# Second FFN of a hybrid decoder step: 8 of 22 columns for the prompt beside decode, 14 as block products for all tokens

## The chip, the cores and the metric

The kernel runs on one NeuronCore of one Trainium2 chip, as one program in one launch. The metric is the device time of one execution in microseconds. Five engines work side by side, each through its own queue in order: TensorE (PE, with its weight loads as PEld), VectorE (DVE), ScalarE (ACT), GpSimd (POOL) and SyncE (SP, which here only issues DMAs). PSUM, into which TensorE writes, has banks of 512 fp32 columns for each of 128 partitions.

## The reference, cut to what matters

One layer for 512 prompt tokens and 32 sample tokens (8 sequences of 4) that share all weights. The model width is 1024, the FFN width 2816.

```python
def swiglu(x, wg, wu, wd):
    return (jax.nn.silu(x @ wg) * (x @ wu)) @ wd

def layer(h, ...):
    h = h + 0.5 * rmsnorm(swiglu(rmsnorm(h, norm_g[0]), wg[0], wu[0], wd[0]), norm_g[1])
    m, c_kv, k_r, s_fin = mixer(rmsnorm(h, norm_g[2]), ...)   # HGRN2 heads and latent attention, then @ w_out
    h = h + rmsnorm(m, norm_g[3])
    h = h + 0.5 * rmsnorm(swiglu(rmsnorm(h, norm_g[4]), wg[1], wu[1], wd[1]), norm_g[5])
    return h, c_kv, k_r, s_fin
```

The mixer's attention runs for prompt tokens over the 512 prompt tokens, and for the samples over 4096 cached tokens each, fetched by pages ("decode"). All inputs and outputs are fp32. The change is about the last line but one, the second FFN, and about the product with `w_out` ahead of it.

## The kernel before, in words

Activations stand transposed: 128 features on the partitions, tokens along the free axis, 8 such slabs for 1024 features. A "column" is 128 of the 2816 FFN features, so there are 22. To keep fp32 accuracy with the faster fp32r matmuls every operand is split into a high and a low part, and each product of two 128-row slabs is three matmuls, high by high, high by low and low by high (`mm3`, `gemm`, `gemm_q`). A weight of 128 columns is fetched as `wraw`, split by ScalarE (high, a cast) and VectorE (low, a subtraction) into `wh` and `wl` (`weight`, L250 and L251), and used by 24 matmuls for each group of tokens.

The stages in order:

- First FFN (to about 385 us). The tokens are two halves of 272 (`even`). Columns 0 to 3 are made plainly (`classic`). From then on two columns at a time are made by `seven`: gate (or up) of two columns for two token halves, with the 1024 features in two parts, is a 2 by 2 by 2 block product that takes seven block products in place of eight, 84 matmuls in place of 96, at the price of sums of weight blocks (L609 to L615), sums of token blocks (`T1` to `T4`, made once, L685) and sums of results (`plus`, L627). Finished columns are multiplied with `w_down` in steps of `down`, which `fill` puts between the block products.
- Mixer projections and the HGRN heads, then attention of the prompt in two halves of 256 queries. The prompt's first half is projected with `w_out` (`project(0)`) between the attention heads. The tokens are here two parts of 256 and 288 (`halves`): the second has 256 prompt tokens and the 32 samples.
- Decode. `decode()` walks through 16 half sequences; for each it gathers pages by indirect DMA on POOL's queue into seven slots, transposes them on VectorE (L1381), makes scores on TensorE in 64x32 tiles (L1393), takes the softmax, and multiplies with the values in column groups of 32 (L1426). Between two of its steps the generator `gb` is advanced: it is `ffn(1, 5, (0,), ...)`, the second FFN of the first 256 tokens, all 22 columns in four groups, gate, up and then down.
- After decode, `decode_end` merges the parts of the softmax and finishes the samples' attention (L1494 to L1515). Then `project(1)` projects the other 288 tokens with `w_out`, with the rest of `gb` between its columns, and `gB`, a second `ffn(1, 5, (1,), ...)`, makes the 22 columns for these 288 tokens, fetching and splitting all its weights a second time. `Finish` turns the prompt part back to rows and stores it.

The order of each engine's instructions is made when the program is built. A planner takes the instructions in the order in which they are traced as their priority, models when each is ready, and puts on every engine the first one that is; `tc.issue_after` holds an instruction behind a named one on the same engine. So a generator that is advanced later has a lower priority, and fills gaps that the planner sees.

The lines that the change touches:

## Time and profile before

| what | value |
|---|---|
| time, median of 3 runs | 1250.78 us (1250.63 to 1252.65) |
| span of the profiled execution | 1241.4 us; the trace gives no other time of its own |
| TensorE busy | 1215.0 us, 98% |
| VectorE busy | 982.7 us, 79% |
| ScalarE busy | 738.8 us, 60% |
| mean granted TensorE clock | 0.999 |
| DMA traffic | 195.59 MB, mean 158 GB/s |

The span goes from the first to the last instruction of one profiled execution; the device time is some 9 us longer. "Busy" is time in which at least one instruction of the engine is under way, so pipelined matmuls count once. In lists of groups the columns are: line, engine, operation, output tile `<-` input tiles, shapes, count, busy time in us, mean length in ns, idle time ahead of them and what ended it. Tiles of the `act` pool are named by their slot (`ha`, `mb`, `uha`), whatever stands in them.

### The profile page before, as it was taken

Reading aid. Unit: us, or ns where it says so; the run is one execution under the profiler, and the core shown is the slowest. Engines: PE = TensorE matmul, PEld = TensorE weight load, DVE = VectorE, ACT = ScalarE, POOL = GpSimd, SP = SyncE. Lnnn points to the kernel's source line nnn. Section 1 sums busy time; section 2 is a strip of 40 time slices with the busy share of each in tenths; the row PEclk is TensorE's granted clock in tenths of the full one; section 3 lists DMA queues with packets and bytes.
Section 4 is the critical chain, followed back from the end, with each engine's and each line's share of the span. In section 5 each row is a group of like instructions: output and inputs, shape, how many; then the busy total and the mean of one; then the engine's idle time right before and its main releaser. Section 6 shows DMA issues by size and latency. Waiting matters only on the chain.

```text
span 1241.4 us, 29997 instructions
## 1 busy us (share of the span) xinstructions
PE 1215.0 (98%) x12366; PEld 1151.3 (93%) x12366; DVE 982.7 (79%) x1976; ACT 738.8 (60%) x1559; POOL 76.5 (6%) x80
## 2 busy tenths in 40 slices
PE   8999999999999999999999999999999999999997
PEld 6999999999999989988898888888888999999997
DVE  7897788878678888786877899999998778566665
ACT  7675545455366744545758766666656776554455
POOL 0000000000000000000001312322310000000000
PEclk9999999999999999999999999999999999999999
DMA  6232333232264213333233868878776635545451
GB/s 238 86 115 90 103 103 102 86 99 91 62 221 147 82 54 105 88 94 130 85 105 117 339 214 303 310 282 323 258 275 232 198 106 188 184 137 188 150 151 60
DMA packets 73113, 195.59 MB, mean 158 GB/s; under 512 B 12336, under 2 KB 27728, under 8 KB 68240
## 3 DMA queue, kind: packets, MB, share of 16 engines
q1 hardware_dynamic: 64512, 150.47, 37.3%
q0 software_dynamic: 7168, 41.95, 9.2%
q8 instruction: 97, 1.59, 0.5%
q10 hardware_dynamic: 1296, 1.26, 0.3%
q14 instruction: 40, 0.33, 0.1%
HBM read 183.97 MB, written 9.67 MB: 156 GB/s over the span
## 4 chain that ended last, share of the span: by engine, by line
PE 79%; DVE 11%; ACT 7%; issue 2%; DMA 2%; SPq 0%; DVEq 0%; ACTq 0%
PE acc L259 29%; PE acc L277 13%; PE dn L259 8%; PE Y L575 7%; PE X L575 4%; PE Z L575 4%; DVE kh L1381 3%; PE acc L731 3%; DVE wl L251 2%; ACT wh L250 1%; PE s L1393 1%; ACT pbuf L1417 1%; DMA wraw<-w_g 1%; PE pa L952 1%; PE o L1426 1%
## 5 line engine op out<-in xcount | busy, mean ns | idle before, releaser
L250 ACT CAST wh<-wraw 128x1024 fp32r<-128x1024 f32 (+2 forms) x194 | 185.0, 957 | 164.3 <-PE acc L259 103.7
L251 DVE TENSOR_TENSOR wl<-wraw,wh 128x1024 fp32r<-128x1024 f32 (+2 forms) x194 | 214.6, 1108 | 72.2 <-ACT wh L250 71.6
L277 PE MATMUL acc<-uha,wh 128*128 128x256 f32 (+1 forms) x528 | 155.5, 295 | 0.1
L277 PE MATMUL acc<-uha,wl 128*128 128x256 f32 (+1 forms) x528 | 150.0, 285 | 0.8 <-DVE wl L251 0.7
L277 PE MATMUL acc<-ula,wh 128*128 128x256 f32 (+1 forms) x528 | 150.5, 286 | 0.0
L259 PE MATMUL acc<-uhb,wh 128*128 128x288 f32 (+1 forms) x432 | 128.0, 296 | 0.0
L259 PE MATMUL acc<-uhb,wl 128*128 128x288 f32 (+1 forms) x432 | 127.0, 295 | 1.0 <-DVE wl L251 0.8
L259 PE MATMUL acc<-ulb,wh 128*128 128x288 f32 (+1 forms) x432 | 127.5, 295 | 0.0
L277 PEld LDWEIGHTS acc<-uha,wh 128*128 128x128 f32 x528 | 99.2, 188 | 8.8 <-issue 7.9
L277 PEld LDWEIGHTS acc<-uha,wl 128*128 128x128 f32 x528 | 99.2, 188 | 2.3 <-DVE wl L251 1.6
L277 PEld LDWEIGHTS acc<-ula,wh 128*128 128x128 f32 x528 | 99.4, 188 | 1.6 <-issue 1.2
L259 PEld LDWEIGHTS acc<-uhb,wl 128*128 128x128 f32 x432 | 81.2, 188 | 1.6 <-DVE wl L251 1.6
L259 PEld LDWEIGHTS acc<-uhb,wh 128*128 128x128 f32 x432 | 81.0, 187 | 0.2 <-ACT uhb L170 0.2
L259 PEld LDWEIGHTS acc<-ulb,wh 128*128 128x128 f32 x432 | 81.1, 188 | 0.1
L259 PE MATMUL dn<-hh,dh 128*128 128x272 f32 x256 | 74.3, 290 | 0.0
L259 PE MATMUL dn<-hh,dl 128*128 128x272 f32 x256 | 73.7, 288 | 0.0
L259 PE MATMUL dn<-hl,dh 128*128 128x272 f32 x256 | 73.6, 288 | 0.0
L277 PE MATMUL acc<-uhb,wh 128*128 128x272 f32 x176 | 52.8, 300 | 0.0
L1417 ACT COPY pbuf<-pt 32x64 f32<-32x64 f32 x192 | 46.5, 242 | 10.1 <-DVE pt L1413 7.3
L259 PE MATMUL acc<-hlb,wh 128*128 128x288 f32 x176 | 52.1, 298 | 0.0
L259 PE MATMUL acc<-hhb,wh 128*128 128x288 f32 x176 | 51.8, 298 | 0.0
L1393 PE MATMUL s<-kh,q 64*32 64x128 f32 x2560 | 48.0, 273 | 3.5 <-DVE kh L1381 3.5
(632 smaller groups left out, 3881.3 us busy)
## 6 DMA issues: line engine op xcount, KB each, us to landing
wraw<-w_u SPq DMA_DIRECT2D x66, 512.0 KB, 4.3
wraw<-w_g SPq DMA_DIRECT2D x65, 512.0 KB, 3.9
wraw<-w_d SPq DMA_DIRECT2D x40, 384.0 KB, 3.5
wraw<-w_in SPq DMA_DIRECT2D x24, 512.0 KB, 3.5
wraw<-w_d SPq DMA_DIRECT2D x32, 320.0 KB, 3.1
wraw<-w_d SPq DMA_DIRECT2D x16, 512.0 KB, 3.8
wraw<-w_o SPq DMA_DIRECT2D x16, 512.0 KB, 3.7
g_S<-state SPq DMA_DIRECT2D x4, 512.0 KB, 4.4
```

What stands on the lines that cost most here:

```text
L250: nc.scalar.copy(wh[:, :kt], w[:, :kt])
L251: nc.vector.tensor_tensor(wl[:, :kt], w[:, :kt], f32(wh[:, :kt]), op=ALU.subtract)
L259: nc.tensor.matmul(out, a, b, start=n == 0, stop=n == last)
L277: nc.tensor.matmul(acc[:, :n], a[:, k], b[:, k], start=k + i == 0, stop=k == kt - 1 and i == 2)
L575: nc.tensor.matmul(bank, a[p][:, k], b[q][:, k], start=first and k + n == 0, stop=k == 3 and n == 2, skip_group_check=True)
L731: nc.tensor.matmul(accs[x, d], wts[d][p][:, k], hs[k // 2][q][:, k % 2, x], start=k + n == 0, stop=k == nf - 1 and n == 2)
L952: nc.tensor.matmul(po[es, c].rearrange("p (n m) -> p n m", m=m), kx[:, cs], up(qx[:, cs], m), start=True, stop=True, skip_group_check=True)
L1381: nc.vector.transpose(kh[:, g].rearrange("p a j k -> p a (j k)"), src)
L1393: nc.tensor.matmul(self.s[r][c * 32 : c * 32 + 32, :P], q[rs, j], kh, start=st + jj == 0, stop=st == len(JS) - 1 and jj == 1, skip_group_c ...
L1417: (nc.scalar.copy if g else nc.vector.tensor_copy)(self.p[g * 32 : g * 32 + 32, c // 2, c % 2 * 4 : c % 2 * 4 + 4, self.i * 16 : self.i * ...
L1426: nc.tensor.matmul(o[g : g + 32, :R], self.p[:, c, a], self.craw[c][:, a], start=i + c == 0 and a < 4, stop=i + c == 2 and a >= 4, skip_gr ...
```

## The change

The second FFN is cut by columns, not by token halves.

- Columns 0 to 7 are made for the 512 prompt tokens beside decode, by the new generator `phase_a`. It starts with `project(1)` for the prompt's second half of 256, makes column 0 for each half by itself, and the others with 512 tokens in one matmul. After four columns their share of down is made, copied from PSUM by ScalarE and stored to DRAM (`mA[0]`, `mA[1]`). The pace is given by `PRE` (two or three steps for each of the first ten decode steps) and then one step for each; it was 100 steps spread evenly.
- The samples' `w_out` and columns 0 to 7 are made apart, in plain fp32, by `rowprod`: the 32 samples are the stationary operand, four weights go through four column groups at once. Their weights come by `rows4` on POOL's DMA queue, unsplit, 2 MB at a time into two slots. `w_out` is done in `decode_end`, the columns in `sample_cols`, which is advanced after each piece of the later columns.
- Columns 8 to 21 are made for all 544 tokens, after decode, in halves of 272 with the block products of the first FFN, which are now a function `block_ffn` for both: columns 8 and 9 plainly, 10 to 21 by `seven`. The token sums T1 to T3 are made from the split u. The gate's result is multiplied with the norm's factor in `gated`.
- The sums of down are put together by DMA: `mA[0]` is loaded into `mT`, `mA[1]` and the parked sums of columns 8 to 11 (`mA[2]`) are added to it by accumulating DMAs on POOL's queue.
- `Finish` works on the second half of 272 (240 prompt tokens as two overlapping blocks of 128, and the samples); the first 272 tokens are stored transposed.
- Outputs of the prompt's attention are split into high and low as they are made (`oo`) instead of ahead of `project`; the four-buffer rotation of `wh` and `wl` becomes two buffers.

```diff
-FCH = (((0, 6), (6, 6), (12, 6), (18, 4)), ((0, 6), (6, 6), (12, 5), (17, 5)))
+FA, CA = 8, 4
...
-NW, WX = 2, 2
-NDEC = 100
+NW = 2
+PRE = (2, 2, 2, 2, 2, 2, 2, 2, 3, 3)
...
+    def block_ffn(i, B, r=None):
+        b11, b21, b22, t1, t2, t3, t4 = B
...
         def gated(H, G, V, i):
             z = G[:, 2 * i : 2 * i + 2]
             t = mk([P, 2, W2], F32, "sit", 2)
+            if r is not None:
+                nc.vector.tensor_tensor(z, z, r, op=ALU.mult)
             sigmoid(t, z)
...
+    def phase_a():
...
+        def gate(f):
+            s = mk([P, TP], F32, "sil", 2, pool=ffa)
+            z = yield from col(wt(w_g, f), f)
+            yield
+            swish(s, z, full)
+            return s
+
+        def up(f, s):
+            z = yield from col(wt(w_u, f), f)
+            yield
+            nc.vector.tensor_tensor(s, s, z, op=ALU.mult)
+            split(hh[:, f % CA], hl[:, f % CA], s)
+
+        def downs(c):
+            for d in range(KD):
+                acc = yield from gemm_q(weight([wcols(w_d[1], c * CA, CA, d * P)], CA), (hh, hl), 2)
+                t = mk([P, TP], F32, "sit", 2, pool=ffa)
+                nc.scalar.copy(t, acc)
+                nc.scalar.dma_start(mA[c][:, d], t)
+                yield
+
+        acc = squares(0)
+        pj = project(1, oo[1], to_ffn, ffa)
+        next(pj)
...
-                nc.scalar.copy(oT[x][:, NH + hd, : 2 * P], o[:, : 2 * P])
+                split(*[t[:, NH + hd] for t in oo[x]], o[:, : 2 * P])
...
-        slots = ("ulb", "uhb", "ha", "hb", "mb", "q0", "dx")
+        slots = ("ma", "dx0", "dx1", "mb", "ha", "hb", "q0")
...
+        def rows4(w, d0, n, slot):
+            out = []
+            for i, sl in enumerate(slot):
+                t = qt[:, : 2 * KD * P] if sl == "q0" else mk([P, 2 * KD * P], F32, sl, pool=act)
+                t = t.rearrange("p (i k c) -> p i k c", i=2, k=KD)
+                nc.gpsimd.dma_start(t, w[d0 + 2 * i : d0 + 2 * i + 2, :, :n].rearrange("i p k c -> p i k c"))
+                out += [t[:, 0], t[:, 1]]
+            return out
+
+        def rowprod(a, raws):
+            o = ps("sr")[:, :P]
+            for k in range(KD):
+                for g in range(4):
+                    nc.tensor.matmul(o[g * TS : (g + 1) * TS], a[:, k], raws[g][:, k], start=k == 0, stop=k == KD - 1, skip_group_check=True)
+            return o
...
+            wo = [rows4(w_o, 0, KD, ("ha", "hb")), rows4(w_o, 4, KD, ("q0", "ma"))]
...
+            tok = tmp("rs_t", 2 * P)
+            for r in range(2):
+                nc.scalar.copy(tok[:, r * P : (r + 1) * P], rowprod(oTs, wo[r]))
+                yield
...
+            split(u4[0][:, :, TP:], u4[1][:, :, TP:], uS)
...
+        def sample_cols():
+            uS, uR = smp
+            z = tmp("rs_t", 2 * P)
+            for r in range(2):
+                nc.scalar.copy(z[:, r * P : (r + 1) * P], rowprod(uR, rows4(w_g[1], 4 * r, KD, ("ma", "mb"))))
+                yield
...
         ga, gn = decode(), decode_new()
-        na, ib = len(JS) * (NH2 + 2) + 4, 0
-        for ia in range(na):
+        for ia in range(len(JS) * (NH2 + 2) + 4):
             next(ga)
             if ia % 2:
                 next(gn, None)
-            while ib * na < (ia + 1) * NDEC:
+            for _ in range(PRE[ia] if ia < len(PRE) else 1):
                 next(gb)
-                ib += 1
         for _ in ga:
             pass
-        decode_end()
+        for _ in decode_end():
+            for _ in range(2):
+                next(gb, None)
...
+        def tile_pair(j, src, C, mid=None):
+            if j == J0:
+                ws = [wsplit(w) for w in raw_pair(src, 2 * j)]
+                for x in BOTH:
+                    classic(ws, C, x, ucol)
+                    next(sc, None)
+                if mid:
+                    mid()
+            else:
+                seven(raw_pair(src, 2 * j), C, mid)
+                next(sc, None)
...
+            if j == 7:
+                mT = [actslot("m", x, n=W2) for x in BOTH]
+                for i in range(2):
+                    for x in BOTH:
+                        n = min(even[x].stop, TP) - even[x].start
+                        (nc.gpsimd.dma_start if i else nc.sync.dma_start)(mT[x][:, :, :n], mA[i][:, :, even[x].start : even[x].start + n], **({"accum_op": ALU.add} if i else {}))
+            if j == 8:
+                fill(99)
+                owed[0] = 0
+                for x in BOTH:
+                    nc.gpsimd.dma_start(mT[x], mA[2][:, :, even[x]], accum_op=ALU.add)
+            tile_pair(j, w_g[1], G)
+            if j == J0:
+                X, Y, Z = (mk([P, 4, W2], F32, n, 3) for n in ("hh", "hl", "hh"))
+                for o, b in ((X, B12), (Y, B11)):
+                    nc.vector.tensor_tensor(o, f32(b[0]), f32(b[1]), op=ALU.add)
+                nc.vector.tensor_tensor(Y, X, Y, op=ALU.subtract)
...
+            def rest():
+                if j > J0:
+                    gated(H, *late, 1)
+                if j in (6, 8):
+                    fill(99)
+                    owed[0] = 0
+                    downs.append(down(j - 2, hs, park if j == 6 else add_m))
+
+            tile_pair(j, w_u[1], V, rest)
```

More of the change, by code (lines that the diff above doesn't have):

```diff
@@ L586, in fill, with down @@
                     downs.pop(0)
[L588 removed]
+        def down(q0, hs, sink):
             nf = 2 * len(hs)
@@ L784, in project @@
             nc.scalar.copy(mT[:, d], acc)
             scale_sq(sacc, mT, d, gv, 3)
+        d0 = 0
+        if pool:
+            for d, acc in enumerate((yield from gemm_2([wo(d) for d in range(2)], o))):
+                column(d, acc)
+            d0 = 2
+            yield
+        for d in range(d0, KD):
+            column(d, (yield from gemm_q(wo(d), o, 4)) if pool else gemm(wo(d), o))
             yield
         yield from post(x, mT, sacc, None, nxt)
+    u4 = []
+    hs2 = dr.tile([P, KD, T], F32, name="hs2", tag="hs2")
```

595 lines of the change are left out of this document (329 added, 266 removed).

## The prediction, made before the changed kernel was run

> **What bounds the kernel now.** I read the page's busy times and chain first, then one row for each stage, then the spacing of TensorE's instructions by width.
>
> ```profile
> span 1241.4 us, 29997 instructions
> PE 1215.0 (98%) x12366; PEld 1151.3 (93%) x12366; DVE 982.7 (79%) x1976; ACT 738.8 (60%) x1559; POOL 76.5 (6%) x80
> PE 79%; DVE 11%; ACT 7%; issue 2%; DMA 2%; SPq 0%; DVEq 0%; ACTq 0%
> ```
>
> The stages (columns: time, busy time and count of PE, PEld, DVE, ACT, POOL, granted clock, DMA share, GB/s) are the first FFN, mixer and HGRN, attention, decode, and the tail after decode.
>
> ```profile
> 5.00:385.00 380.00, 379.37 (x2990) 374.22 (x2991) 303.63 (x557) 216.16 (x407) 0.56 (x1) 1.00 0.35 115
> 385.00:573.00 188.00, 187.65 (x1932) 171.29 (x1931) 151.51 (x354) 100.14 (x222) 1.88 (x8) 1.00 0.30 91
> 573.00:698.00 125.00, 118.70 (x867) 109.72 (x866) 94.84 (x229) 89.50 (x208) 8.47 (x8) 1.00 0.43 144
> 698.00:951.00 253.00, 248.28 (x4463) 218.39 (x4465) 237.73 (x522) 159.37 (x419) 64.06 (x58) 1.00 0.78 276
> 951.00:1241.40 290.40, 281.04 (x2124) 277.70 (x2124) 194.23 (x315) 171.42 (x304) 1.35 (x1) 0.99 0.51 158
> ```
>
> TensorE sets the end in every stage: it is idle 4.7 us of the decode stage and 9.4 us of the tail. The change touches these last two, 543 us of the span. VectorE is second: 94% in decode, 67% in the tail.
>
> A busy matmul overlaps the next, so its mean length isn't its price. The price is the spacing: the time of a stretch of one kind over its count (windows, then steps of the chain of waits).
>
> ```profile
> 609.00:614.30 5.30, 5.30 (x25) 4.33 (x24) 4.54 (x8) 5.11 (x9) 0.00 (x0) 1.00 0.38 129
> 100.00:300.00 200.00, 200.00 (x1591) 199.32 (x1590) 158.24 (x291) 101.93 (x192) 0.00 (x0) 1.00 0.31 96
> 1040.00:1220.00 180.00, 180.00 (x1347) 179.45 (x1347) 111.38 (x163) 94.90 (x153) 0.00 (x0) 1.00 0.52 160
> ...
> 954.33 8.75 PE acc L277 x73
> ...
> 753.97 1.86 PE o L1426 x32
> 763.09 1.52 PE s L1393 x96
> ```
>
> 288 wide (second half of the tokens): 180/1347 = 0.1336 us. 272 wide (first FFN): 200/1591 = 0.1257. 256 wide: 8.75/73 = 0.1199. 512 wide: two of the 25 were under way when the window opened, so 5.30/23 = 0.2304; its bounds are 5.30/25 = 0.212 and twice the 256 wide, 0.240. Column groups in fp32 (four at a time, 32 columns each) with 256 moving columns: 32 in 1.86 us. The sample products move 128: between half of that, 0.93, and the whole. The 64x32 products of L1393 do move 128, eight at a time, 96 in 1.52; four at a time that is 1.01 for 32. I take 1.0.
>
> **What the change removes and adds on TensorE.** Removed: the first half's 22 columns, 22 x 8 x 3 = 528 matmuls each for gate, up and down, 1584 x 0.1199 = 189.9 us; the second half's 1584 and the 192 of its output projection, 1776 x 0.1336 = 237.3. Together 427.2.
>
> Added beside decode: output projection of the second prompt half 192 x 0.1199 = 23.0; first column by halves 96 x 0.1199 = 11.5; the other seven columns 7 x 2 x 24 = 336 and eight columns of down, 2 x 8 x 4 x 3 = 192, 528 x 0.2304 = 121.7. Added after decode: columns 8 and 9 plainly, 192; twelve block products of 84 in place of 96, 1008; down of 14 columns, 14 x 8 x 2 x 3 = 672; 1872 x 0.1257 = 235.3. Samples: eight products of 32 matmuls, two each for w_out, gate, up and down, 8.1, and about 2 for sums and turns. Together 401.6. **Net -25.6 us.** Twelve saved matmuls in each of twelve pairs x 0.1257 are 18.1 of it; wide matmuls, even halves and samples left out of eight columns are the rest.
>
> **The decode stage.** The groups by line over 700 to 955 us, and a window:
>
> ```profile
> L251 DVE TENSOR_TENSOR wl<-wraw,wh 128x1024 fp32r<-128x1024 f32 (+2 forms) x64 | 70.0, 1096 | 10.7 <-ACT wh L250 10.4
> L336 DVE TENSOR_TENSOR sil<-sil,sit 128x256 f32<-128x256 f32 x19 | 7.9, 421 | 2.5 <-ACT sit L322 2.1
> L392 DVE TENSOR_TENSOR ma<-ma,acc 128x256 f32<-128x256 f32 x16 | 6.4, 402 | 0.0
> ...
> 712.00:951.00 239.00, 234.40 (x4350) 205.10 (x4346) 223.89 (x493) 149.97 (x398) 56.15 (x53) 1.00 0.77 273
> ```
>
> VectorE loses 64 weight splits (70.0), four operations of each of 19 columns (4 x 7.9 = 31.6) and 6.4 of sums; it gains 24 splits of 1024 at 1.22 and 16 of 512 at 0.69 (rows below) = 40, four 512-wide operations in each of eight columns, 22, and about 17 of the projection. That is 29 less, so up to 4.7 us of TensorE's idle time could go; I take 2 (0 to 4.7). Fetched bytes fall as well. Against it: 22 steps now run before the first scores, and the second prompt half waits for the projection's norm, about 11 us of VectorE and ScalarE in series behind 48 matmuls (5.8) of the other half. I take +2 (0 to 6). The extra split of each attention output moves from the tail into the attention stage; its eight pieces of some 0.4 us hide beside TensorE there, or add at most 3.
>
> **The samples' chain.** Decode ends now with a chain that other matmuls cover (timeline, then chain):
>
> ```profile
> 951.51 0.70 PE L1494 MATMUL pb<-q,ones 128*128 128x256 f32 x2
> 953.70 0.63 PE L1434 MATMUL o<-q,q 128*128 128x32 f32 x4 [0.91 <-ACT q L1429]
> 954.59 0.22 DVE L1435 COPY q<-o 128x64 f32<-128x64 f32 x1
> ...
> 963.08 1.82 PE o L1514 x16
> ```
>
> L1494 stands later in the program than L1434 and runs before it: the planner orders each engine by readiness, so independent matmuls can be put into gaps. The chain takes 964.9 - 951.5 = 13.4 us. Behind it now come two w_out products, a turn, two norms and the split of u: 2.0 plus some 16 dependent steps of about 0.5, estimated from the 0.22 to 0.70 above, 10 us. Cover: the last five steps of down, 30 x 0.2304 = 6.9; columns 8 and 9 of the first 272 tokens, which hold no sample, 96 x 0.1257 = 12.1; the chain's own matmuls 4. So 23.4 against 23.0. I take 2; without the 12.1, because the planner leaves them behind, 12.
>
> **The block stage's first pairs.** By form, from 40 to 380 us, where the first FFN does the same:
>
> ```profile
> L171 DVE TENSOR_TENSOR sl<-wraw,sh 128x512 fp32r<-128x512 f32 x36 | 23.6, 686 | 0.7
> L609 DVE TENSOR_TENSOR S<-wraw 128x512 f32<-128x512 f32 x18 | 12.3, 685 | 0.0
> L627 DVE TENSOR_TENSOR ha<-Y,tq 128x272 f32<-128x272 f32 x27 | 11.7, 434 | 0.8 <-PE Y L575 0.8
> L657 DVE TENSOR_TENSOR ha<-ha,sit 128x544 f32<-128x544 f32 x22 | 15.9, 722 | 4.9 <-ACT sit L322 4.9
> L685 DVE TENSOR_TENSOR ma<-ma,mb 128x1088 f32<-128x1088 f32 x1 | 1.3, 1280 | 0.0
> L251 DVE TENSOR_TENSOR wlx<-wraw,whx 128x1024 fp32r<-128x1024 f32 x2 | 2.4, 1218 | 0.0
> ...
> 60.70:71.50 10.80, 10.80 (x86) 10.63 (x85) 9.27 (x16) 10.24 (x20) 0.00 (x0) 1.00 0.27 100
> 71.50:83.00 11.50, 11.50 (x94) 11.50 (x93) 11.27 (x22) 7.88 (x16) 0.00 (x0) 1.00 0.29 93
> ```
>
> A block product costs TensorE 84 x 0.1257 = 10.6 us and VectorE 11 x 0.685 + 5 x 0.434 = 9.7, and the gate now has a fourth operation, for the norm: 4 x 0.72 = 2.9. That is 12.6 against 10.6 wherever no down runs beside it. The two windows show such a pair in the first FFN: VectorE 20.5 of 22.3 us, TensorE without a gap. In the new stage three and a half products in a row have no down. Before them the token combinations (12 operations x 1.28 = 15.4) can start only when the samples are in. From that point VectorE has 15.4 + 3.5 x 9.7 + 4 x 2.9 = 61; TensorE 12.1 + 3.5 x 10.6 + 6.1 of sample products = 55. I take 6 us; 0 if work prepared ahead covers it, 14 if the combinations, 12.8 to the one that the second block wants, aren't covered. After that down (1.5 us a step against 0.8 of VectorE) restores TensorE's lead.
>
> **The sample weights and the parked sums.** POOL's queue now carries the 4 MB of w_out and six loads of 2 MB into the same two slots, each issued only after the product before it has read them; the accumulating loads of the parked sums stand behind these. From the DMA view:
>
> ```profile
> hb<-hsp SPq DMA_DIRECT2D x1, 1152.0 KB, 9.0
> ...
> ha<-hs SPq DMA_DIRECT2D x1, 1024.0 KB, 5.7
> ...
> hb<-pool_c,idx POOLq DMA_INDIRECT x4, 9.4
> ```
>
> 1 MB lands in 5.7 to 9.4 us beside other traffic; two at once I put at 9. The program leaves 48 matmuls, 6.0 us, between the first four sample products, so three of them can be 3 us late; TensorE runs in order, and the block products behind a late one wait. I take 3 (0 to 15). The Trainium skill's "DMA: Bandwidth & Descriptors" (Anatomy of one DMA) fits one such transfer at 2.0 us plus its bytes over 436 GB/s; 2 MB would be an estimated 6.8 us by it, and the three waits 2 us together, not 9. The rows above are slower than the page. The accumulating loads have a whole block product ahead of their first reader: 1 (0 to 6). The last columns and the finish keep their form: no change.
>
> **Sum.** 1241.4 - 25.6 + 2 - 2 + 2 + 6 + 3 + 1 = 1227.8 of span. The trace shows no own time beside the span; the median of the runs, 1250.78, is 9.4 above it, which I add: **1237 us**.
>
> **Rivals.** *All of it arrives.* The planner hides every new wait, as it did in the first FFN (379.37 of 380.00 busy): 1250.8 - 25.6 - 2 = 1223. Against it: combinations that can't start before the samples. *Decode keeps its own pace.* If VectorE and the gathers, not TensorE, pace the scores (94% busy speaks for it), the 33 us of projection and first column, 15 us of them more than ran there before, come ahead of a decode that isn't shorter: 1237 + 15 = 1252, no change. Against it: 29 us less on VectorE. *The sample columns pace the tail* (slower). Sixteen MB come through two slots in series; if the planner believes them earlier than they land and sets them ahead of the block products, w_out's second half and the first four products wait about 6 us each (9 + 3 of turnaround - 6.0), 30, and the uncovered chain costs 10 more. Less the 5 that my sum has for both: 1237 - 5 + 40 = 1272; it decides from 16 us of such waits over my sum on. For it: the order is fixed at build time. Against it: four slots of w_out come free before decode ends.
>
> By "TensorE: Matmul & The Clock Gate" (What's actually happening) of the Trainium skill, an idle window of some 3.4 us halves the clock until a busy one follows. The trace grants 1.00 in all but the tail's last microseconds, so it doesn't show this; after each long wait of the slower rival it would add an estimated 1.7 us.
>
> **How the numbers follow.** A measurement of this kernel tells 0.2%, 2.5 us, from no change. My forecast, 1227 to 1247: 0.56. All of it arrives: 0.15. Decode keeps its pace: 0.09. The sample columns pace the tail: 0.20. Faster 0.71, same 0.09, slower 0.20. The range goes from 1221, all saved with decode's idle time gone, to 1257, where half of the slower rival's waits occur.
>
> **What would show it.** Right: the decode stage ends 3 to 10 us earlier; a spacing near 0.126 in the block stage; TensorE idle 8 to 15 us between the last attention value and the second block pair, with VectorE as releaser; a tail of 265 to 280 us in place of 290. Wrong: waits of TensorE on the sample weights over 10 us together, a decode stage over 253 us, or 512-wide matmuls spaced above 0.24.

## The result, and the profile after

The changed kernel is slower: 1267.99 us (1267.38 to 1269.21) against 1251.72 us for the kernel before on the same chip, a ratio of 1.0125 (95% interval 1.0108 to 1.0142). The forecast was 1237, a ratio of 0.989.

From the page of the profiled execution (span, engines, chain):

```profile
span 1265.6 us, 29473 instructions
PE 1223.2 (97%) x12244; PEld 1122.7 (89%) x12244; DVE 981.6 (78%) x1992; ACT 703.3 (56%) x1524; POOL 91.2 (7%) x102
PE 79%; DVE 10%; ACT 5%; DMA 4%; issue 2%; SPq 0%; DVEq 0%; ACTq 0%
```

That execution took 1267.38 us, 1.8 above its span. So the 9.4 us that the prediction laid around the span was no cost of the program. On four other chips, which ran all the experiments, the kernel before takes 1243.5 to 1244.6 us, some 2 to 3 above the 1241.4 of its profile: so that profile was very likely taken on a chip of their speed, and the first chip is 0.6% slower. The changed kernel was therefore profiled again on one of the four (span 1256.5, time 1258.28; the run e5 below). This second profile stands beside the one of before from here on, and the forecast for such a chip reads 1227.8 + 1.8 = 1229.6 us against a measured 1258.4. Some 29 us are missing. One run of e4 (1476.46 us at a mean granted clock of 0.75) and one of the kernel before (1303.85 us at 0.849) stand apart from all others and are left out of the comparisons.

The stages of the second profile (columns as in the prediction: time, PE, PEld, VectorE, ScalarE, POOL, granted clock, DMA share, GB/s), then the stretches in which time is lost:

```profile
5.00:385.00 380.00, 379.66 (x2984) 374.73 (x2985) 302.43 (x554) 215.35 (x406) 0.92 (x3) 1.00 0.35 115
385.00:573.00 188.00, 187.66 (x1934) 171.45 (x1932) 151.67 (x354) 100.81 (x223) 1.53 (x6) 1.00 0.30 90
573.00:701.00 128.00, 124.32 (x917) 116.17 (x913) 99.86 (x238) 89.93 (x205) 4.92 (x5) 1.00 0.37 114
701.00:955.50 254.50, 241.85 (x3893) 183.45 (x3893) 209.72 (x467) 146.53 (x403) 69.42 (x67) 0.99 0.75 262
955.50:1256.50 301.00, 282.17 (x2524) 273.99 (x2523) 214.94 (x378) 148.55 (x287) 15.70 (x17) 0.97 0.52 159
...
701.00:748.20 47.20, 40.15 (x276) 36.56 (x275) 37.32 (x72) 31.87 (x69) 10.18 (x8) 0.93 0.83 293
748.20:955.50 207.30, 201.70 (x3618) 146.89 (x3618) 172.40 (x395) 114.67 (x334) 59.24 (x59) 1.00 0.73 255
955.50:1000.00 44.50, 42.23 (x461) 38.51 (x461) 34.42 (x49) 17.12 (x33) 3.46 (x5) 0.88 0.55 193
1000.00:1151.00 151.00, 144.04 (x1309) 141.03 (x1308) 109.25 (x194) 80.75 (x157) 10.85 (x12) 0.99 0.68 197
...
703.90:710.70 6.80, 5.04 (x22) 4.78 (x23) 6.16 (x15) 4.25 (x11) 5.11 (x4) 0.50 1.00 344
973.50:983.70 10.20, 9.87 (x43) 9.73 (x44) 7.86 (x11) 2.46 (x6) 0.00 (x0) 0.50 0.26 84
```

The same places before: attention to the first score, the first score to the last value, the chain after decode.

```profile
698.00:711.50 13.50, 13.37 (x109) 12.93 (x107) 13.33 (x30) 8.90 (x21) 7.91 (x5) 1.00 0.83 310
711.50:951.50 240.00, 235.40 (x4360) 205.56 (x4359) 224.39 (x493) 150.97 (x400) 56.15 (x53) 1.00 0.77 273
951.50:1000.00 48.50, 47.53 (x373) 46.78 (x370) 35.16 (x62) 34.70 (x67) 0.00 (x0) 1.00 0.68 223
```

Decode itself is shorter, 207.3 us in place of 240.0. But it starts 36.7 us later, and the tail is 301.0 in place of 290; the forecast's tail was 265 to 280. TensorE's idle time and its clock name three places. What a stretch at half clock costs is read from the spacing of the matmuls in it: 256-wide ones start 0.213 us apart there and 0.120 elsewhere, 272-wide ones 0.227 and 0.126. From 701 to 748 TensorE is idle 7.05 us and runs 6.8 us at half clock; the 20 matmuls of `project(1)` in that stretch lose some 1.9 us. After decode it is idle 2.3 and has 10.2 us at half clock, in which 28 wide and 16 narrow matmuls lose some 4.4. In the block stage (1000 to 1151) it is idle 7.0, and a stretch of 3.4 us from 1130.6 on, right behind a wait, costs some 1.5. Before, the first of these places cost 0.1 us and the second 1.0, and the clock was full until the last microseconds.

### The profile page after: what moved, and what is told of

It is laid out like the page before. It is cut to its first block, busy times and chain, and to the rows that moved or that the text cites. A ratio compares the mean times of both kernels' runs of the same rounds, so it can differ in the third digit from the quotient of the medians.

```text
span 1265.6 us, 29473 instructions
## 1 busy us (share of the span) xinstructions
PE 1223.2 (97%) x12244; PEld 1122.7 (89%) x12244; DVE 981.6 (78%) x1992; ACT 703.3 (56%) x1524; POOL 91.2 (7%) x102
## 4 chain that ended last, share of the span: by engine, by line
PE 79%; DVE 10%; ACT 5%; DMA 4%; issue 2%; SPq 0%; DVEq 0%; ACTq 0%
PE acc L246 19%; PE acc L228 11%; PE dn L228 10%; PE Y L447 8%; PE Z L447 6%; PE X L447 5%; PE s L1391 3%; PE acc L627 3%; PE acc L1800 2%; PE o L1424 2%; DVE kh L1379 1%; DMA wraw<-w_u 1%; PE pa L957 1%; DMA wraw<-w_g 1%; ACT pbuf L1415 1%
## 5 line engine op out<-in xcount | busy, mean ns | idle before, releaser
L246 PE MATMUL acc<-uh,wh 128*128 128x272 f32 (+2 forms) x496 | 161.1, 325 | 0.7 <-ACT uh L195 0.7
L246 PE MATMUL acc<-ul,wh 128*128 128x272 f32 (+2 forms) x496 | 155.7, 315 | 0.7 <-DVE ul L196 0.7
L246 PE MATMUL acc<-uh,wl 128*128 128x272 f32 (+2 forms) x496 | 155.3, 314 | 0.5 <-DVE wl L220 0.5
L220 DVE TENSOR_TENSOR wl<-wraw,wh 128x1024 fp32r<-128x1024 f32 (+2 forms) x80 | 86.2, 1078 | 35.8 <-ACT wh L219 33.4
L219 ACT CAST wh<-wraw 128x1024 fp32r<-128x1024 f32 (+2 forms) x80 | 74.8, 935 | 67.1 <-PE acc L246 49.3
L228 PE MATMUL dn<-hh,dh 128*128 128x272 f32 x384 | 111.4, 290 | 0.0
L228 PE MATMUL dn<-hh,dl 128*128 128x272 f32 x384 | 110.5, 288 | 0.0
L228 PE MATMUL dn<-hl,dh 128*128 128x272 f32 x384 | 110.5, 288 | 0.0
L246 PEld LDWEIGHTS acc<-uh,wh 128*128 128x128 f32 x496 | 93.2, 188 | 14.1 <-issue 9.1
L246 PEld LDWEIGHTS acc<-uh,wl 128*128 128x128 f32 x496 | 93.1, 188 | 7.0 <-issue 1.3
L246 PEld LDWEIGHTS acc<-ul,wh 128*128 128x128 f32 x496 | 93.3, 188 | 6.2 <-issue 1.2
L228 PEld LDWEIGHTS dn<-hh,dh 128*128 128x128 f32 x384 | 72.3, 188 | 1.0 <-issue 0.2
L228 PEld LDWEIGHTS dn<-hl,dh 128*128 128x128 f32 x384 | 72.5, 189 | 0.0
L228 PEld LDWEIGHTS dn<-hh,dl 128*128 128x128 f32 x384 | 72.1, 188 | 0.0
```

Source lines behind the costliest of these rows:

```text
L219: nc.scalar.copy(wh[:, :kt], w[:, :kt])
L220: nc.vector.tensor_tensor(wl[:, :kt], w[:, :kt], f32(wh[:, :kt]), op=ALU.subtract)
L228: nc.tensor.matmul(out, a, b, start=n == 0, stop=n == last)
L246: nc.tensor.matmul(acc[:, :n], a[:, k], b[:, k], start=k + i == 0, stop=k == kt - 1 and i == 2)
```

## The experiments

All runs are compared with the kernel before on the same chip. Times of different chips stand side by side below, because the kernel before agrees on these chips within 1.2 us. The expectations of e1 to e4 count from the first chip's 1267.99, so their differences are what is compared. The 95% intervals reach 1.4 to 3.8 us to either side, and by the ratios the gains come out up to 3.5 us smaller than by the medians; a gain below some 4 us is therefore not told from none. Executions of one kernel differ in part by their clock: e1's four take 1249.94 us at a mean granted clock of 0.995, 1252.58 and 1254.57 at 0.992, and 1257.66 at 0.990.

### A control, and cover for the samples' chain

e5 is the changed kernel as it is.

> The changed kernel itself, beside the runs of the kernel before on the chip that ran the first four experiments' fellow kernels, because the two profiles come from chips that differ (the kernel before took 1251.7 us on the one and 1243.5 on the other). Theory (the change's own losses, independent of the chip): 1.0125 times the kernel before, between 1.010 and 1.015. Rival (a good part of the loss belongs to the first chip, whose decode bursts show gaps of 0.59 us): 1.006 or less.

1258.44 us, ratio 1.0107 (1.0089 to 1.0125). The loss belongs to the kernel and not to the first chip.

e1 keeps some ten steps of `gb` back for the time of the samples' chain:

```diff
-            for _ in range(PRE[ia] if ia < len(PRE) else 1):
+            for _ in range(PRE[ia] if ia < len(PRE) else int(ia % 8 < 7)):
```

> Edit: after the first ten decode steps one step in eight is skipped, so about ten more steps of the first eight columns (14 us of TensorE) are left for the samples' chain after decode. Theory A (TensorE runs dry in the samples' chain, and its clock is halved there for 10 us): decode ends about 14 us earlier, the chain gets no longer, the half clock after decode goes; 8 to 14 us less than the changed kernel, 1254 to 1260. Rival B (the chain's length isn't what costs; the sample products and their loads are): the same work only moves, 1266 to 1269.

1253.57 us, ratio 1.009 (1.0068 to 1.0111), 4.9 below the changed kernel by the medians and 2.1 by the ratios, whose intervals overlap. The mechanism of theory A is seen below, its 8 to 14 us are not. The chain of the second profile (start, duration, what) shows what was missing there:

```profile
956.87 6.82 PE acc L246 x29
963.69 1.71 PE o L1553 x16
965.40 3.63 PE sr L1492 x128
969.03 0.27 PE tp L1498
```

The 30 wide matmuls of down that were left, 6.8 us, ran before the chain's first long step. None was left beside the norms, and the first product of columns 8 and 9 (`acc`, L228), on which the prediction had counted for cover, started only after it, at 973.8 us, ended by the split of its own weight:

```profile
968.96 0.33 PE L1498 MATMUL tp<-ident,rs_t 128*128 128x128 f32 x1
969.44 0.33 PE L1498 MATMUL tp<-ident,rs_t 128*128 128x128 f32 x1 [0.15 <-ACT rs_t L1558]
970.25 1.97 PE L1507 MATMUL pr<-s_post,ones 128*128 128x32 f32 x16 [0.47 <-ACT s_post L1563]
973.83 0.60 PE L228 MATMUL acc<-uh,sh 128*128 128x272 f32 x1 [1.62 <-ACT sh L158]
```

With e1's extra steps in the chain the clock stays whole, in the profiled execution, which is the fastest of the four:

```profile
943.00:990.00 47.00, 45.47 (x434) 38.93 (x426) 27.46 (x40) 20.48 (x39) 2.81 (x4) 1.00 0.72 250
```

### The clock by itself

e8 puts eight matmuls that nobody reads into each of six steps of the chain:

```diff
-        for _ in decode_end():
+        for n, _ in enumerate(decode_end()):
...
+            if n > 1:
+                dm = ps("dm", "pm")
+                for i in range(8):
+                    nc.tensor.matmul(dm[:, :256], u4[0][:, i, :P], u4[1][:, i, :256], start=i == 0, stop=i == 7)
```

> Adds eight matmuls of 256 columns, whose result nobody reads, to each step of the samples' chain at decode's end, so that TensorE is not quiet for long; 64 or so in all, 0.12 us each, some 8 us if none of them fell into idle time. Theory 1 (after decode TensorE runs at half the granted clock for 10.2 us, and it is the quiet chain that halves it): the granted clock stays at 1.00 through the chain, and the time is 0 to 5 us below the changed kernel although work was added. Theory 2 (the chain's dependencies set the time, the clock doesn't matter): 0 to 8 us above the changed kernel with the clock at 1.00.

```profile
963.00:1000.00 37.00, 36.41 (x474) 33.89 (x474) 27.59 (x35) 13.68 (x29) 3.51 (x5) 1.00 0.48 156
```

The clock is 1.00 through the chain, so it is the quiet chain that halves it. The time is 1261.60 us, 3.2 more, which is in the range of the second theory. Up to the first block product the 48 dummies (about 48 x 0.12 = 5.8 us) cost about as much as the clock gave back: it starts 57.1 us after the last value against 56.8 (both read from the trace). The rest is lost behind it:

```profile
1000.00:1155.00 155.00, 145.34 (x1298) 142.41 (x1297) 108.85 (x193) 79.51 (x154) 10.06 (x10) 0.97 0.66 192
```

In the block stage TensorE is now idle 9.7 us in place of 7.0, and three stretches of 3.4 us run at half clock in place of one. Why the waits there grew is open. Dummy work didn't pay here; cover should be work that must be done anyway, as in e1, though e1's gain isn't clear of the intervals.

### The start of decode

Two edits of the scores' order and of weight buffers came first. e2 spreads the score groups over the steps:

```diff
-RUNS = {2: (0, 1, 2), 4: (3, 4)}
+RUNS = {1: (0,), 2: (1,), 3: (2,), 4: (3, 4)}
```

> Edit: the five score groups of a half sequence stand behind four decode steps (1, 1, 1 and 2) in place of two (3 and 2). Theory D (with 512-wide matmuls, six instructions a step, a burst of 64 score records outruns what TensorE's sequencer has queued, and it waits about 0.3 us three times a half): the scores' slots fall from 59.6 to about 50 us, 6 to 10 us less than the changed kernel, 1258 to 1262. Rival (the pauses are waits for transposes on VectorE): they stay, 1266 to 1269.

1259.93 us, 1.0136 (1.0118 to 1.0154): no time is won. The gaps of 0.59 us inside the score bursts, at which the edit aimed, stand in the first chip's profile (16 of them); in the second profile of the same kernel the bursts wait in six places, 3.9 us in all, and with e2 nowhere. Losing these waits didn't shorten the program.

e3 gives every third `w_out` weight of `project(1)` a buffer of its own, in the slot of `hl`, which is idle then:

```diff
+            home = None
+            if pool and d % 3 == 2:
+                t = mk([P, 2, 8, P], F32R, "hl", pool=pool)
+                home = t[:, 0], t[:, 1]
-            return weight([wcols(w_o, 0, KD, d * P)], KD)
+            return weight([wcols(w_o, 0, KD, d * P)], KD, home=home)
```

> Edit: every third weight of the second half's output projection gets a buffer of its own (the slot of hl, idle then), three in place of two. Theory A1 (the start of decode loses about 16 us because two weights are held until the last attention output is in, and the next can't be split): TensorE's idle time from 701 to 750 us falls from 7 to 3 or 4 us, the half clock there goes as well, 4 to 8 us less than the changed kernel, 1260 to 1264. Rival (the wait is for the attention output, the norm of the second half, or the 2 MB through the one q0 slot): no more than 1 us, 1267.

1255.37 us, 1.011 (1.0079 to 1.014). The interval covers the changed kernel's ratio. TensorE is idle 4.9 us from 701 to 749 in place of 7.05; of the waits below the one of 1.73 us goes, the others stay, and so does the half clock. In the second profile these gaps, and the waits of the gathers from 701 to 748 us (engine, line, what it waited for, total, times, longest), are:

```profile
704.70 0.77 PE L1331 MATMUL b<-ident,q 128*128 128x128 f32 x2 [1.95 <-DVE mxs L1322]
706.85 0.58 PE L246 MATMUL acc<-ha,wl 128*128 128x256 f32 x1 [0.96 <-DVE wl L220]
719.91 0.39 PE L246 MATMUL acc<-ha,wl 128*128 128x256 f32 x1 [1.73 <-DVE wl L220]
...
POOL ma L1364 <- ACT uh L195: 23.5, 1, 23.5
POOL hb L1364 <- PE acc L246: 18.7, 1, 18.7
```

The gathers find no room: `ma` holds the projection of the first half until its norm (`uh`, L195) is through, `ha` and `hb` hold the second half's attention output until `project(1)` has read it, and `q0` holds its residual. This is why the 22 steps of `PRE` stand beside the first ten decode steps, ahead of the first scores. TensorE has little besides them to do: from 701 to 748 it waits 3.2 us for their weights, 1.4 for the second half's norm and 2.0 for a maximum of the samples' own scores (L1322).

e9 leaves `PRE` empty, one step for each decode step:

```diff
-PRE = (2, 2, 2, 2, 2, 2, 2, 2, 3, 3)
+PRE = ()
```

> One step of the projection and first columns per decode step from the start on, in place of the 22 steps ahead of the first scores; 12 steps are then left beside the samples' chain. Theory 1 (these 22 steps, run without anything beside them, are what empties TensorE at the start of decode): first score 15 to 25 us earlier than at 748 us, less than 4 us of idle TensorE between attention and first score, no half clock after decode; 8 to 12 us less than the changed kernel. Theory 2 (the start waits for what stands before it, the norm of the first half and the slots of the gathers, whatever the order): the idle time at the start stays near 10 us and only the cover of the chain is won, 4 to 5 us less.

1248.68 us, 1.0037 (1.0024 to 1.0049), 9.8 below the changed kernel. In this order the gathers put their rows over the second half's residual and attention output before these are read, so the second prompt half comes out as something else; its time is that of an order for which buffers are lacking. e13 is the nearest one that has room: `ha` and `hb` are gathered into at the same decode step as before, when the 15 steps have run that read them, and `q0` five decode steps later.

```diff
-PRE = (2, 2, 2, 2, 2, 2, 2, 2, 3, 3)
+PRE = (1, 1, 1, 1, 1, 2, 2, 2, 2, 2)
...
-                    if n < 3 and st == 0:
+                    if n < 4 and st == 0:
...
-                        gather(2 + n // 2)
+                        gather(2 - n // 3)
```

> One projection or column step per decode step for the first five, two for the next five, then one; the seventh block's gather moves five decode steps back, behind the last reader of its buffer. Seven steps are left for the samples' chain. Theory 1 (the 22 steps ahead are the cause): first score 15 us or more before 748, 6 to 9 us less than the changed kernel, no half clock after decode. Theory 2 (only the cover counts): 3 to 5 us less.

1251.69 us, 1.0067 (1.0051 to 1.0084), 6.8 less than the changed kernel. From the last attention product to the first score, decode, and after it:

```profile
701.00:731.00 30.00, 26.20 (x182) 24.88 (x183) 22.73 (x44) 21.61 (x46) 8.18 (x7) 0.89 0.90 320
731.00:942.00 211.00, 207.32 (x3670) 152.16 (x3668) 183.99 (x420) 119.92 (x350) 59.36 (x60) 1.00 0.74 258
942.00:990.00 48.00, 45.93 (x437) 40.72 (x437) 31.95 (x45) 20.15 (x38) 2.81 (x4) 0.96 0.71 237
```

The first score is 16.6 us earlier, the idle time ahead of it 3.8 us in place of 7.05, and after decode the clock is 0.96 over the window in place of 0.88; one stretch of 3.4 us at half clock is left there, against the expectation of none. The first score and the time are as the first theory has them. But half of the start's idle time stays, 2.0 us of it in the wait for L1322 shown above, and so do the 6.8 us at half clock (0.89 over the window). So only about half of the gain, 3.3 us of idle time, comes from the start; some 3 come from the clock after decode, where the seven steps left over are cover.

### The samples, the parked sums and the block stage's weights

In the block stage TensorE waits three times, each time for sums of block products on VectorE (`hb`, L496):

```profile
1035.96 0.39 PE L447 MATMUL Y<-uh,wh 128*128 128x272 f32 x1 [2.70 <-DVE hb L496]
1093.89 0.40 PE L447 MATMUL Y<-t4h,wh 128*128 128x272 f32 x1 [1.75 <-DVE hb L496]
1129.61 0.39 PE L447 MATMUL Y<-t4h,sh 128*128 128x272 f32 x1 [2.24 <-DVE hb L496]
```

VectorE is named, but the chain ahead of the first two goes back to weights that were under way for 7 us (the chain of the third runs through matmuls and shows no load), and POOL's queue (start, duration, what) has large loads going at those times:

```profile
1025.34 7.01 DMA wraw<-w_d
...
1077.67 7.69 DMA wraw<-w_g
```

```profile
1021.28 0.70 POOL L1484 DMA_DIRECT2D ma<-w_d  x1 [9.39 <-PE sr L1492]
1021.97 0.71 POOL L1484 DMA_DIRECT2D mb<-w_d  x1
...
1062.41 1.53 POOL L1738 DMA_DIRECT2D ma<-mA  x1 [19.43 <-DMA mb<-mA]
1074.81 1.46 POOL L1738 DMA_DIRECT2D mb<-mA  x1 [10.87 <-PE X L447]
1114.65 1.45 POOL L1743 DMA_DIRECT2D ma<-mA  x1 [38.38 <-DMA mA<-s_post]
```

Three runs take these apart: e6 without the samples' columns 0 to 7, e7 without the six loads of the parked sums (two plain, four accumulating), and e14 with the products but one load for all six.

```diff
-            uS, uR = smp
...
-            nc.scalar.copy(mT[1][:, :, TP - W2 :], back(t))
+            yield
```

> Leaves out the samples' share of columns 0 to 7 (their gate, up and down products and the 12 MB of weights that these fetch); everything else stays. Theory 1 (the products cost what their records show, some 1.9 us each): six products gone, 11 to 12 us less than the changed kernel, and the three gaps of 2 to 3 us in the block stage stay. Theory 2 (their loads also hold back the block stage's weights): 18 to 22 us less, and those gaps are gone. Rival, the prediction's price: 6 us less.

```diff
-                        (nc.gpsimd.dma_start if i else nc.sync.dma_start)(mT[x][:, :, :n], mA[i][:, :, even[x].start : even[x].start + n], **({"accum_op": ALU.add} if i else {}))
+                    nc.gpsimd.memset(mT[x][:, :, : (W2, TP - W2)[x]], 0.0)
...
-                    nc.gpsimd.dma_start(mT[x], mA[2][:, :, even[x]], accum_op=ALU.add)
```

> Leaves out the accumulating loads of the parked down sums of columns 0 to 7 and sets the place they go to to zero; the stores stay. Theory 1 (these loads compete with the block stage's weights): the gaps at 1043 and 1102 us of the changed kernel shrink below 1 us each, 5 to 8 us less time. Theory 2 (the gaps come from the weights' own chain, raw copies in five buffers, with the samples' loads): no change, within 2 us. The prediction's price for the sums was 1 us.

```diff
+            raws = rows4(w_g[1], 0, KD, ("ma", "mb"))
...
-                nc.scalar.copy(z[:, r * P : (r + 1) * P], rowprod(uR, rows4(w_g[1], 4 * r, KD, ("ma", "mb"))))
+                nc.scalar.copy(z[:, r * P : (r + 1) * P], rowprod(uR, raws))
```

> All six sample products of gate, up and down read the first 2 MB of the gate's weights; the other 10 MB aren't fetched, all products stay. Theory 1 (products and loads each cost about half of the samples' 24.9 us): 11 to 14 us less than the changed kernel, the gap at 1033 us gone. Theory 2 (the products are the cost, the loads only make the one gap): 2 to 5 us less. Theory 3 (the loads are nearly all of it, the products hide): 18 us less or more.

| run | us | ratio (95%) | against the changed kernel | waits of TensorE from 1020 to 1135 us that end at VectorE |
|---|---|---|---|---|
| changed | 1258.44 | 1.0107 (1.0089 to 1.0125) | | 2.70, 1.75, 2.24 |
| e6, no samples | 1233.58 | 0.9912 (0.9894 to 0.9929) | -24.9 | 2.86 (the last) |
| e7, no sums | 1251.25 | 1.0050 (1.0032 to 1.0068) | -7.2 | 2.92 (the first) |
| e14, one load | 1250.70 | 1.0057 (1.0040 to 1.0074) | -7.7 | 2.11, 2.64 (the later two) |

So the first wait goes with the samples' loads (e14) and the later two with the loads of the sums (e7); the second goes without the samples' columns too (e6). e7's first theory expected the first wait to go as well, and it stays. Both kinds of load slow the same weights: in the DMA view from 1020 to 1135 us (KB each, median us to landing) the up weights land in 7.6 us in the changed kernel and in 3.7 without the samples, but also in 3.8 in e7 and in 3.6 in e14:

```profile
wraw<-w_u SPq DMA_DIRECT2D x7, 512.0 KB, 7.6
```

```profile
wraw<-w_u SPq DMA_DIRECT2D x7, 512.0 KB, 3.7
```

The samples' eight columns cost 24.9 us, more than e6's second theory had (18 to 22); the prediction had 6 for the six products and 3 for their loads. 7.7 of it is loads (6.2 by the ratios), between the first theory of e14 and its second. The products are the larger part; one by itself, in the chain of the first profile:

```profile
996.86 1.89 PE sr L1492 x64
```

Six of these are 11.3 us. That leaves 24.9 - 7.7 - 11.3 = 5.9 us for the chain from product to product and for what it delays; no run measured that part alone.

e10 takes two of the accumulating loads out, by adding the second sum to the first in DRAM as it is written, beside decode:

```diff
-                nc.scalar.dma_start(mA[c][:, d], t)
+                if c:
+                    nc.gpsimd.dma_start(mA[0][:, d], t, accum_op=ALU.add)
+                else:
+                    nc.scalar.dma_start(mA[0][:, d], t)
...
-                for i in range(2):
+                for i in range(1):
```

> The second parked sum is added to the first in DRAM when it is written, beside decode, so that only two of the four accumulating loads are left in the block stage. Theory 1 (each of the two late gaps belongs to the accumulating loads issued just before it): the gap at 1092 us goes, that at 1127 stays, 2 to 4 us less than the changed kernel. Theory 2 (decode's own transfers, which take 0.73 of the DMA engines, pay for it): no change or up to 3 us more.

1253.90 us, 1.0083 (1.0062 to 1.0105), 4.5 less (3.0 by the ratios, not clear of the intervals); the wait at 1094 is gone and the other two stay, as the first theory has it.

e4 makes columns 10 to 21 by plain products, without block products and without the token sums:

```diff
-                seven(raw_pair(src, 2 * j), C, mid)
+                ws = [wsplit(w) for w in raw_pair(src, 2 * j)]
+                for i in range(2):
+                    for x in BOTH:
+                        acc = ps("acc", "acc")[:, :W2]
+                        mm3(acc, [((ws[i][0][:, k], ws[i][1][:, k]), ucol(x, k)) for k in range(KD)])
```

> Edit: the block products are undone alone; columns 10 to 21 are made plainly for all 544 tokens, eight products in place of seven, without token or weight sums; all else as changed. If TensorE sets the pace of that stage, the 144 matmuls come back, 18 us, less about 9 us of waits for VectorE and weights that go: 1274 to 1280. Rival C (VectorE and the weight loads pace the block stage, so the saved matmuls brought nothing): 1265 to 1270.

1267.59 us, 1.0196 (1.0176 to 1.0217), 9.2 above the changed kernel, which is in the range of the first theory (6 to 12 above) and not of the rival's (at most 2). The block products are worth about that much of the 18.1 us that their count promises. The remainder is near the 7.0 us that TensorE is idle in the block stage; the plain products have no wait over 0.5 us after 1016 us, but ahead of it two of 1.3 and 3.0 us for sample weights (`ma<-w_u`), so 9.2 isn't the block products' worth alone.

### Do the losses add up?

e15 has the order of e13 and no samples in columns 0 to 7; e16 that order and one load.

> The order of the steps as above, and the samples' share of columns 0 to 7 left out. Theory 1 (the two losses are separate): 7 + 25 us less than the changed kernel, 1224 to 1229 us, that is the forecast's 1229.6 less the 6 us that it had for these products. Theory 2 (they overlap): above 1231 us.

1230.35 us, 0.9889 (0.9872 to 0.9905): 28.1 less than the changed kernel, where the single edits give 6.8 + 24.9 = 31.7. It lies between the two theories' ranges, and the 3.5 us that are lacking are about as large as the intervals. The forecast for this kernel, without the 6 for these products and the 3 for their loads, is 1220.6. Of the 9.8 us above it, e7 accounts for 6 (the parked sums are still in it), and half of the start's idle time and clock, some 5, for the rest. But the 1220.6 still holds the forecast's 6 for the first block pairs, which cost nothing without the samples (e6), so some 5 us are not accounted for.

> The order of the steps, and one load for all six sample products. Theory 1: as the sum of the two single edits, within 3 us; by the first theories of both, 1237 to 1241 us, below the kernel before. Theory 2 (both give the same time back): within 3 us of the better single edit.

1247.56 us, 1.0037 (1.0026 to 1.0048): 10.9 less, against 14.5 for the two edits. Again some 3.6 are lacking; neither theory's bound was met exactly, and it stays above the kernel before.

Two combinations were to reach the kernel before. e11 joins e3's buffer, e9's order and e10's sum (its time is again that of an order for which buffers are lacking), e12 the same with e1's cover in place of e9's order.

> Third weight buffer at the start, one step per decode step, and the second sum in DRAM together. Theory 1 (the losses are separate and add up): the gains of the single edits, 3 for the buffer, 8 for the steps and 3 for the sum, so some 14 us less than the changed kernel, equal to the kernel before. Theory 2 (the block stage goes at the pace of its weights, so that what is won ahead of it is partly lost in it): 6 to 9 us less, still 0.4% or more above the kernel before.

> The same three with the other way to leave steps for the chain (one decode step in eight after the tenth takes none). Theory 1: as the sum of the single edits, 3 + 4.5 + 3, some 10 us less than the changed kernel. Theory 2: 5 to 7 us less, because what is won ahead of the block stage comes back as waits for its weights.

1251.43 us (1.0062, 1.0042 to 1.0082) and 1251.60 us (1.0064, 1.0044 to 1.0084), 7 us below the changed kernel each. So e11 isn't better than e9 alone: the block stage has two waits in place of three, of 1.2 and 2.2 us, and e9's three (0.6, 0.7 and 1.8) are as long together. Fewer loads moved the waits here and didn't shorten them, nearer to the second theory.

e17 folds all three parked sums into one in DRAM, with e13's order, and e18 adds a cover of one step in sixteen:

```diff
-            nc.scalar.dma_start(mA[2][:, d, even[x]], t)
+            n = min(even[x].stop, TP) - even[x].start
+            nc.gpsimd.dma_start(mA[0][:, d, even[x].start : even[x].start + n], t[:, :n], accum_op=ALU.add)
...
-                    nc.gpsimd.dma_start(mT[x], mA[2][:, :, even[x]], accum_op=ALU.add)
+                    nc.sync.dma_start(mT[x][:, :, :n], mA[0][:, :, even[x].start : even[x].start + n])
```

> The order of the steps as before, and all three parked sums folded into one in DRAM as they are written, so that the block stage gets one plain load of them in place of three, and nothing but the samples' small part is accumulated on the way in. Nothing is left out. Theory 1 (the losses are separate): 6.75 for the order and 5 to 7 for the sums, 1245 to 1247 us, equal to the kernel before within 0.3%. Theory 2 (they overlap, as order and samples did by 3.5 us): 1248 to 1251 us.

> The same, and one decode step in sixteen takes no column step, so that some five more are left for the samples' chain. Theory 1 (the chain still lacks cover): the half clock of 3.4 us and the gap of 2.3 us after decode go, 2 to 4 us less than the kernel with the order and the sums alone, and equal to the kernel before or up to 3 us below it. Theory 2 (enough cover with seven steps): no change against that kernel.

1258.31 us (1.0119, 1.0104 to 1.0134) and 1257.68 (1.0110, 1.0092 to 1.0127): worse than e13 by 6. That is against both theories of e17; e18's second, no change against e17, holds. The waits haven't gone: the first is still 2.63 us in e17, and one of 2.02 at another product is new,

```profile
1112.26 0.39 PE L447 MATMUL X<-uh,wh 128*128 128x272 f32 x1 [2.02 <-ACT tq L499]
```

and e17's profiled execution (1253.6, at a mean clock of 0.992) is 4.7 us faster than its others (0.988 to 0.990), so that profile doesn't show the whole loss. Why adding in DRAM in the block stage as well gave a longer time is open.

## Why the prediction was wrong

The count of matmuls held: where nothing waits, 512-wide products stand 6.82/29 = 0.235 us apart (0.2304 predicted). The sum failed in its terms for what surrounds them. Predicted and measured, in us on a chip of the second profile's speed:

| term of the sum | predicted | measured | from |
|---|---|---|---|
| eight sample products | 8.1 | 15.0 | 3.63 + 6 x 1.89 |
| start of decode | +2 | +8.8 | idle 7.05 and 1.9 of clock, less 0.1 before |
| attention's extra splits | 0 (to 3) | 0 | 2.5 us longer with 42 matmuls (5.0 us) of `project(1)` taken ahead into it; idle 3.7, before 6.3 |
| decode's idle time | -2 | +1.0 | 5.6 against 4.6 |
| samples' chain | +2 | +5.7 | idle 2.3 and 4.4 of clock, less 1.0 before |
| first pairs of the block stage | +6 | 0 | e6: busy from 1025 to 1095 without a gap |
| sample weights | +3 | 7.7 | e14 |
| parked sums | +1 | 7.2 | e7 |

The differences add up to 25.3 us (6.9 + 6.8 + 3 + 3.7 - 6 + 4.7 + 6.2); 28.8 are missing. The rows of e7 and e14 are uncertain by some 3 us each, the others are read from one profile, and some terms may overlap, as e15 and e16 suggest. The 5.9 us of the samples' columns that no run took apart stand in no row. So the sum names where the time went and doesn't prove the size of each row.

**Sample products.** A mis-sized term. "32 in 1.86 us" was taken from column groups whose records count 32; the fp32 products are recorded twice for each matmul of the program (x64 for the 32 of `rowprod`, x2560 for 1280 scores), so the row priced 16 matmuls and the factor of two was lost. The upper bound given, the whole 1.86, was right: 1.89.

**Start of decode.** "I take +2 (0 to 6)" was the costliest step that failed, beside the sample products. The prediction knew that 22 steps run before the first scores, and put the second half's norm behind 48 matmuls of the first, where it is and costs 1.4 us. It left out TensorE's other waits there, 3.2 us for weights and 2.0 for the samples' own scores, with no score of the decode to run in between because the gathers' slots are the steps' own operands, and it left out the half clock of the quiet stretch. e13's order takes 3.3 us of the idle time away; e9, whose scores start at 706 us, also has 3.4 us at half clock there in place of 6.8. Of the prediction's own signs of being wrong, this one came: a decode stage over 253 us (254.5 from 701 to 955.5).

**Samples' chain.** "23.4 against 23.0" of cover counted the 30 matmuls of down and 96 of columns 8 and 9. The first ran too early, the second came behind, and its own bound for that case was 12. What e1 brought back with ten more steps, 4.9 us by the medians and 2.1 by the ratios, leaves the size open.

**First block pairs.** The mechanism (VectorE behind) was wrong: with the weights on time, e6 has TensorE without a gap while VectorE is busy 87%.

```profile
1025.00:1095.00 70.00, 70.00 (x557) 69.87 (x556) 60.71 (x106) 42.72 (x84) 1.45 (x1) 1.00 0.46 146
```

VectorE does end the waits, as the prediction said it would, but the weights make it late. Had I followed the releaser no further than the first step, it would have looked confirmed.

**Sample weights and parked sums.** Both were priced at their own reader. The longest wait of TensorE for a sample weight is 0.28 us. They cost at the readers of other transfers, the block stage's weights, which the prediction left out: a large load on one queue was weighed against its deadline, and not against the 512 KB loads that share the DMA engines.

**What surrounds the span.** The 9.4 us came from a slower chip's time beside this profile's span, not from the program; 1.8 is right. As a ratio this did no harm.

**The rivals.** "The sample columns pace the tail" gave the side and, at 1272, the time nearest to 1268, but not by its mechanism: the waits of some 6 us on the samples' weights don't occur, so its nearness is luck. "Decode keeps its own pace" is half right: the 33 us come ahead of decode, yet decode is shorter by 32.7. The sentence on the clock, set aside because the trace of before grants 1.00, was the one that bore on this change. "TensorE: Matmul & The Clock Gate" (What's actually happening) of the Trainium skill says that an idle window of some 3.4 us halves the clock; the stretches at half clock here are 3.4, 6.8 and 10.2 us long, whole windows, so the trace agrees, with the length of the window. It differs in two things: the longest gap ahead of the stretch at 973.5 is the 1.62 us shown above, so partial idleness is enough; and by the rule a busy window brings the full clock back, but there it stayed at half for three windows in which TensorE was busy 9.87 of 10.2 us. By the spacing, the two stretches shown cost some 6.3 of their 17.0 us.

## What to carry to other kernels

Work that is moved out of a shared pass has to pay for its own latency: 32 samples rode along with 256 other tokens at 288 - 256 = 32 columns a matmul, and alone they cost products, a second fetch of 12 MB and a chain. Price a new transfer at every other transfer that is in flight with it, and follow a wait past the engine that ends it to what made that engine late. Before a stage is moved ahead of another, list which buffers the second needs that the first still holds; the order of the steps follows from that.

## What the runs showed of the hardware

- An fp32 matmul of the program stands in the trace as two records (64 for the 32 of `rowprod`); the fp32r ones stand as one. Counts of the two kinds can't be compared without it.
- The sample products' 64 records take 1.89 us, 0.0295 each on average. In the trace four of them, one for each column group, start some 0.007 us apart and the next four 0.11 us after the first. For the value products, which move 256 columns in place of 128, it is 0.22. So the moving columns set the price here, not the number of instructions:

```profile
996.92 0.28 PE L1492 MATMUL sr<-ma,sq 128*32 128x128 f32 x2
997.03 0.28 PE L1492 MATMUL sr<-ma,sq 128*32 128x128 f32 x2
```

- The Trainium skill's "TensorE: Matmul & The Clock Gate" (Wait — 56ns, not 53.3ns?) gives a floor of some 25 ns from start to start. The records of different column groups don't keep to it: they start 7 ns apart.
- The clock is halved in whole stretches of 3.4 us and can stay so while TensorE has work; 272-wide matmuls then start 0.227 us apart in place of 0.126. 48 dummy matmuls keep it up through the chain and win no time (e8).
- The same program takes 1251.7 us on one chip and 1243.5 to 1244.6 on four others, three times what the forecast called measurable.
- An accumulating load of 1088 KB into SBUF takes 11.3 and 15.1 us, a plain one of the same size 7.5 in the same stretch. They go by different queues and meet different traffic (in e13 960 KB took 9.5 us plain and 10.8 accumulating), so the price of accumulating itself isn't taken apart:

```profile
ma<-mA POOLq DMA_DIRECT2D x2, 1088.0 KB, 15.1
mb<-mA POOLq DMA_DIRECT2D x1, 1088.0 KB, 11.3
ma<-mA SPq DMA_DIRECT2D x1, 1088.0 KB, 7.5
```
